# A two-layer hybrid-attention kernel: the products that feed its output projections are issued behind finished tiles

## The chip, the cores and the metric

The kernel runs on one core of one Trainium2 chip. The metric is the device time of one execution in microseconds (us), the median over several executions. Engines are named as the profile names them: PE (matrix multiply), DVE (vector), ACT (scalar activation), POOL (GpSimd) and SP, whose only work here is to issue DMA transfers.

## What is computed

The reference is a backbone of two layers over 2048 latent tokens and 256 context tokens, width 1024. Layer 0 runs windowed grouped-query attention beside latent attention, layer 1 neighbourhood attention on a grid. Both end in the same way, and only that end is touched by the change. Cut to it:

```python
o = attention(...)                     # (tokens, 1024), softmax denominators divided out
o = o * silu(z)                        # a gate path, the same width
h = h + gate * (o @ w_out)             # gate: one row for latent, one for context tokens
# after layer 1:  out = rms_norm(h, final_norm)
```

## The kernel before

`outp(l)` is the output projection of layer `l`. The attention stage has left three arrays in device memory, all laid out as channels by tokens: `o` as two halves that must be added, `z` (the gate values) and `rd` (reciprocals of the softmax denominators, one row for 64 channels). What the matmuls need is `(o_a + o_b) * rd * z`, split into a high part and a rest, for the 8 blocks of 128 channels.

The tokens are taken in chunks of 512: four and a half chunks in layer 0 (18 tiles of 128 tokens), four in layer 1 (16 tiles). `gsteps(c)` gives the steps for chunk `c`: `load(j)` issues, on SP, the transfers of block `j` (512 KB of `o`, 256 KB of `z`, twice 128 KB of `rd`), `ahead` says how many blocks the loads run in front, and `comp(j)` does the arithmetic: an add (L1188), a multiply by `rd` (L1189), a multiply by `z` (L1190), all on DVE, then a copy to the high part on ACT (L1192) and the rest on POOL (L1193). In chunk 0 of layer 1 the add and the first multiply run on POOL, since that chunk is prepared under the attention of layer 1. Layer 1 keeps its blocks in a ring of four buffers (`slots`), layer 0 in two or three buffers per array.

A tile is 48 matmuls (`product`, L1227: 8 blocks, three terms, two halves of the width) into one of four PSUM tiles `y`. A finished tile is multiplied by the gate (L1252) and added to the residual rows `rx` (L1253), both on DVE. In layer 0 SP then stores it (`s_h`, L1255). In layer 1 it is also normalised: squares with their sum on ACT (L1259), the root on POOL (L240, L241), a last multiply on DVE (L1261), then the store (L1262). In layer 0 DVE also works off the steps of `mod_rows` here (L207: products of `adat`, loaded through two buffers, with a row `scb`), which give the modulation of the next layer.

In the source the `comp`s of chunk `c+1` are spread over the tiles of chunk `c`. The order in which each engine issues them is not the source's: a scheduler picks, engine by engine, among the instructions that its own estimate says are ready. `tc.issue_after(x)` adds a rule to it: what is written under it comes behind `x` in the order of an engine, where both run on that engine. The hardware then follows that order strictly, with semaphores for the data.

The lines of the last context of layer 0's attention matter too: a reduction, a reciprocal and a small copy on DVE (L1061, L716 and `dnsb`, L720) make the last denominators, on which the last matmuls of chunk 0 wait.

## Time and profile before

| | us |
|---|---|
| time before, median of 3 runs | 3604.93 (3603.82 to 3609.08) |
| the profiled execution | 3600.51 |
| its span, first to last instruction | 3598.7 |
| PE busy in the span | 3452.3 (96%) |
| DVE / ACT / POOL busy | 2300.2 / 1901.1 / 1754.1 |

The profile is of one execution, so the times of a step are taken from it and the sum is set against its 3600.51 us. The span leaves out what lies before the first and behind the last instruction, 1.8 us. Line numbers of the rows are those of the kernel before.

### The profile page before, as it was taken

How to read it: one execution, taken by the hardware profiler on the slowest of the kernel's cores; microseconds unless marked ns; L12 is line 12 of the kernel's file. 1: busy time of each engine (PE TensorE's matmuls, PEld its weight loads, DVE VectorE, ACT ScalarE, POOL GpSimd, SP SyncE). 2: the span in 40 equal slices, each digit the busy share in tenths (PEclk: the TensorE clock that was granted, in tenths of full speed). 3: DMA queues.
4: the chain of work that ended last, by engine and by line, in shares of the span. 5: the costliest groups of instructions: out<-in, count | busy, mean ns of one | idle time of the engine just before them, and what ended most of it. 6: DMA issues, size and time to landing. Idle time of an engine off the chain costs nothing.

```text
span 3598.7 us, 53026 instructions
## 1 busy us (share of the span) xinstructions
PE 3452.3 (96%) x17607; PEld 2858.7 (79%) x17607; DVE 2300.2 (64%) x4305; ACT 1901.1 (53%) x3808; POOL 1754.1 (49%) x1656
## 2 busy tenths in 40 slices
PE   7899999999999999999989989999999999999988
PEld 6788878889877777777668768888888899999766
DVE  6545742489999999999968852203110188888565
ACT  4343432499777777777731132223222288888511
POOL 6465653211499999999962342224113134333532
PEclk9999999999999999999989989999999999999999
DMA  7757663852331232321269754544345567666685
GB/s 246 228 187 263 191 184 121 265 144 72 82 70 24 57 71 70 70 46 45 58 188 326 243 167 161 166 115 149 128 131 151 182 252 257 239 226 229 199 243 167
DMA packets 381052, 576.77 MB, mean 160 GB/s; under 512 B 35393, under 2 KB 218081, under 8 KB 370913
## 3 DMA queue, kind: packets, MB, share of 16 engines
q1 hardware_dynamic: 380777, 573.39, 52.2%
q8 instruction: 138, 2.26, 0.3%
q14 instruction: 137, 1.12, 0.1%
HBM read 399.36 MB, written 173.90 MB: 159 GB/s over the span
## 4 chain that ended last, share of the span: by engine, by line
PE 70%; DMA 9%; DVE 5%; issue 3%; ACT 2%; POOL 1%; SPq 1%; DVEq 0%; ACTq 0%; POOLq 0%
PE mm L276 7%; PE mm L278 7%; PE mm L277 7%; PE co L697 5%; PE ptc L688 4%; PE bo L1041 3%; PE bm L984 3%; PE bs L1020 3%; PE bo L1042 3%; PE bs L1021 3%; PE bs L1022 3%; PE ao L697 2%; PE pta L688 2%; DMA ord<-s_rd 1%; PE y L1227 1%
## 5 line engine op out<-in xcount | busy, mean ns | idle before, releaser
L270 POOL TENSOR_TENSOR wl<-ws,wh 128x512 fp32r<-128x512 f32 (+2 forms) x320 | 420.6, 1332 | 667.1 <-ACT wh L269 566.8
L1031 POOL TENSOR_TENSOR bacc<-bacc,bph 128x512 f32<-128x512 f32 (+1 forms) x528 | 667.4, 1266 | 34.5 <-ACT bph L1025 1.6
L1025 ACT ACTIVATE bph<-bs 128x512 fp32r<-128x512 f32 (+1 forms) x610 | 353.5, 579 | 214.8 <-PE bs L1022 183.0
L986 DVE TENSOR_REDUCE bmx<-bm 128x1 f32<-128x512 f32 (+1 forms) x656 | 406.0, 627 | 58.8 <-PE bm L984 42.4
L1027 DVE TENSOR_TENSOR bpl<-bs,bph 128x512 fp32r<-128x512 f32 (+1 forms) x610 | 400.1, 658 | 15.7 <-ACT bs L1026 14.8
L1026 ACT ACTIVATE bs<-bs 128x512 f32<-128x512 f32 (+1 forms) x610 | 350.8, 575 | 0.0
L276 PE MATMUL mm<-Uh,wh 128*128 128x512 f32 (+1 forms) x832 | 324.2, 391 | 4.6 <-ACT Uh L368 4.6
L1494 POOL TENSOR_TENSOR cbias<-cbu,rm 128x384 f32<-128x384 f32 x144 | 158.4, 1113 | 344.5 <-DVE cnm L1523 202.7
L277 PE MATMUL mm<-Ul,wh 128*128 128x512 f32 (+1 forms) x832 | 323.6, 389 | 0.0
L278 PE MATMUL mm<-Uh,wl 128*128 128x512 f32 (+1 forms) x832 | 321.3, 389 | 0.0
L1523 DVE CUSTOM_DVE_ANT_0 cp<-cs,cbias 128x640 f32<-128x640 f32 (+1 forms) x256 | 222.5, 886 | 138.6 <-PE cs L1519 91.9
L269 ACT ACTIVATE wh<-ws 128x512 fp32r<-128x512 f32 (+2 forms) x328 | 194.8, 613 | 207.8 <-DMA ws<-in_w_dram 174.3
L1041 PE MATMUL bo<-bph,bv 128*128 128x512 f32 (+1 forms) x610 | 240.4, 394 | 15.5 <-ACT bos L1046 15.5
L1020 PE MATMUL bs<-bqh,bkh 97*128 97x512 f32 (+1 forms) x610 | 242.5, 398 | 12.2 <-DVE bpl L1027 11.5
L249 DVE TENSOR_TENSOR plc<-ptc,phc 128x512 fp32r<-128x512 f32 (+1 forms) x384 | 234.8, 640 | 15.2 <-ACT phc L248 14.6
L984 PE MATMUL bm<-bkh,bqh 96*128 96x512 f32 (+1 forms) x656 | 241.4, 383 | 2.0 <-DVE bmx L986 1.7
L1042 PE MATMUL bo<-bpl,bv 128*65 128x512 f32 (+1 forms) x610 | 236.0, 387 | 3.3 <-DVE bos L1048 3.3
L1021 PE MATMUL bs<-bql,bkh 96*128 96x512 f32 (+1 forms) x610 | 238.3, 391 | 0.0
L1022 PE MATMUL bs<-bqh,bkl 96*128 96x512 f32 (+1 forms) x610 | 236.7, 388 | 0.0
L248 ACT ACTIVATE phc<-ptc 128x512 fp32r<-128x512 f32 (+1 forms) x384 | 205.4, 559 | 55.8 <-PE ptc L688 55.6
L1528 ACT ACTIVATE cp<-cp,cnm 128x640 f32<-128x640 f32 (+1 forms) x256 | 226.0, 883 | 16.2 <-DVE cnm L1523 15.8
L688 PE MATMUL ptc<-ident,cp 128*128 128x128 f32 x1408 | 205.4, 273 | 0.2 <-ACT cp L1528 0.2
(314 smaller groups left out, 8757.5 us busy)
## 6 DMA issues: line engine op xcount, KB each, us to landing
ws<-in_w_dram SPq DMA_DIRECT2D x256, 256.0 KB
ck<-s_kcT SPq DMA_DIRECT2D x32, 1152.0 KB
cv<-s_vc SPq DMA_DIRECT2D x64, 512.0 KB
adat<-in_adat_dram SPq DMA_DIRECT2D x96, 256.0 KB
o<-s_o SPq DMA_DIRECT2D x40, 512.0 KB
s_z<-zs SPq DMA_DIRECT2D x64, 256.0 KB
s_qcT<-st SPq DMA_DIRECT2D x64, 256.0 KB
s_kcT<-st SPq DMA_DIRECT2D x32, 512.0 KB
```

Of the source, the lines that this page charges most:

```text
L270: (eng or nc.gpsimd).tensor_sub(l[:, :w], s[:, :w], f(h[:, :w]))
L276: nc.tensor.matmul(out, a[0], b[0], start=first, stop=False)
L277: nc.tensor.matmul(out, a[0], b[1], start=False, stop=False)
L278: nc.tensor.matmul(out, a[1], b[0], start=False, stop=last)
L688: nc.tensor.transpose(ps[:, col : col + P], src(), ident)
L984: nc.tensor.matmul(ps[:, :w], t["qh"][0:96, b * P : (b + 1) * P], t["kh"][0:96, k0 : k0 + w], start=True, stop=True)
L986: nc.vector.tensor_reduce(t["mx"][:, j : j + 1], ps[:, :w], AX.X, ALU.max)
L1020: nc.tensor.matmul(ps[:, :n], t["kh"][0:97, ks], t["qh"][0:97, qs], start=True, stop=False)
L1025: nc.scalar.activation(hi[:, :n], ps[:, :n], AF.Exp)
L1026: self.acts = nc.scalar.activation(ps[:, :n], ps[:, :n], AF.Exp).ins
L1027: nc.vector.tensor_sub(lo[:, :n], ps[:, :n], f(hi[:, :n]))
L1031: self.pools = nc.gpsimd.tensor_add(st["acc"][:, :n], f((st["h0"] if j == 1 else st["acc"])[:, :n]), f(hi[:, :n])).ins
```

## The change

Three edits, all in `outp`:

```diff
-            ahead = (1 if l else 0, 2 if l else 1)
+            ahead = (1 if l else 0, 3 if l else 1)
+
+            done = []
...
-                    e1.tensor_add(a, a, o[:, 1, :n])
-                    e1.tensor_mul(a, a, rd[:, 0, :n])
-                    nc.vector.tensor_mul(a, a, z[:, 0, :n])
-                    h, lo = [x[:, j % 4, :n] for x in (G[c][0][j // 4], G[c][1][j // 4])]
-                    nc.scalar.activation(h, a, AF.Copy)
-                    nc.gpsimd.tensor_sub(lo, a, f(h))
+                    with ExitStack() as behind:
+
+                        for ins in done:
+                            behind.enter_context(tc.issue_after(ins))
+                        e1.tensor_add(a, a, o[:, 1, :n])
+                        nc.vector.tensor_mul(z[:, 0, :n], z[:, 0, :n], rd[:, 0, :n])
+                        nc.vector.tensor_mul(a, a, z[:, 0, :n])
+                        h, lo = [x[:, j % 4, :n] for x in (G[c][0][j // 4], G[c][1][j // 4])]
+                        nc.scalar.activation(h, a, AF.Copy)
+                        nc.gpsimd.tensor_sub(lo, a, f(h))
...
-                nc.vector.tensor_add(y, y, x)
+                done[:] = [nc.vector.tensor_add(y, y, x).ins]
...
-                    nc.scalar.activation(junk, y, AF.Square, accum_out=ss)
+                    done.append(nc.scalar.activation(junk, y, AF.Square, accum_out=ss).ins)
                     r = self.rstd(p, ss, D, "o")
-                    nc.vector.scalar_tensor_tensor(y, y, r, fg, ALU.mult, ALU.mult)
+                    done[0] = nc.vector.scalar_tensor_tensor(y, y, r, fg, ALU.mult, ALU.mult).ins
```

- A `comp` that the source writes behind a tile is now issued behind that tile's last DVE instruction (in layer 1 its ACT copy also behind the tile's squares). The `comp`s of chunk 0 stand ahead of any tile and are not tied.
- In layer 1 the loads of a chunk's blocks run three in front, not two.
- `z` is multiplied by `rd` first, then `o` by that product, both on DVE. In chunk 0 of layer 1 this takes eight multiplies from POOL to DVE. Elsewhere the count of instructions stays: 17609 rows on PE, 3322 on ACT and 2008 transfers before and after.

The scheduler answers with another order. In the changed kernel L1194, L1195 and L1196 are the add and the two multiplies, L1258 and L1259 the tile's gate and residual, L1267 the last multiply of layer 1. Names are the program's: `ry00` is tile 0 of layer 0, `oo010`, `oz010`, `ord010` the arrays of block 0 of chunk 1 of layer 0, `o114` block 4 of chunk 1 in layer 1.

DVE, layer 0, the last denominators of the attention stage. Before:

```order
L1061 TENSOR_REDUCE denb7_1536_21225<-bdt7_12_21226 128x4
L716 RECIPROCAL denb7_1536_21225<-denb7_1536_21225 128x4
L207 SCALAR_TENSOR_TENSOR mj1_000_21615,mcol0_21609<-adat1_0_0_21610,scb0_21606 128x512
L207 SCALAR_TENSOR_TENSOR mj1_010_21617,mcol0_21609<-adat1_0_0_21610,scb0_21606 128x512
L207 SCALAR_TENSOR_TENSOR mj1_100_21621,mcol0_21609<-adat1_1_0_21612,scb0_21606 128x512
L207 SCALAR_TENSOR_TENSOR mj1_110_21623,mcol0_21609<-adat1_1_0_21612,scb0_21606 128x512
L1188 TENSOR_TENSOR oo013_21564<-oo013_21564 128x512
L720 COPY dnsb7_1536_21235<-dnb7_1536_21233 4x128
```

The same place after:

```order
L1061 TENSOR_REDUCE denb7_1536_21225<-bdt7_12_21226 128x4
L716 RECIPROCAL denb7_1536_21225<-denb7_1536_21225 128x4
L207 SCALAR_TENSOR_TENSOR mj1_000_21615,mcol0_21609<-adat1_0_0_21610,scb0_21606 128x512
L207 SCALAR_TENSOR_TENSOR mj1_010_21617,mcol0_21609<-adat1_0_0_21610,scb0_21606 128x512
L207 SCALAR_TENSOR_TENSOR mj1_100_21621,mcol0_21609<-adat1_1_0_21612,scb0_21606 128x512
L207 SCALAR_TENSOR_TENSOR mj1_110_21623,mcol0_21609<-adat1_1_0_21612,scb0_21606 128x512
L207 SCALAR_TENSOR_TENSOR mj1_200_21627,mcol0_21609<-adat1_2_0_21619,scb0_21606 128x512
L720 COPY dnsb7_1536_21235<-dnb7_1536_21233 4x128
```

Nine instructions on blocks 0 to 2 of chunk 1 stood directly ahead of L1061 before; after, the last of chunk 0's stands there. Between L1061 and `dnsb` there are now five L207 and no block.

DVE, layer 0, the border from chunk 0 to chunk 1. Before:

```order
L1188 TENSOR_TENSOR oo017_21643<-oo017_21643 128x512
L1189 TENSOR_TENSOR oo017_21643<-oo017_21643,ord017_21645 128x512
L207 SCALAR_TENSOR_TENSOR mj1_500_21729,mcol0_21609<-adat1_5_0_21721,scb0_21606 128x512
L1190 TENSOR_TENSOR oo017_21643<-oo017_21643,oz017_21644 128x512
L207 SCALAR_TENSOR_TENSOR mj1_510_21731,mcol0_21609<-adat1_5_0_21721,scb0_21606 128x512
L1252 TENSOR_TENSOR ry00_21523<-y00_21376,gate0_21265 128x1024
L207 SCALAR_TENSOR_TENSOR mj1_600_21735,mcol0_21609<-adat1_6_0_21727,scb0_21606 128x512
L1188 TENSOR_TENSOR oo020_21822<-oo020_21822 128x512
L1252 TENSOR_TENSOR ry01_21560<-y01_21377,gate0_21265 128x1024
L1253 TENSOR_TENSOR ry00_21523<-ry00_21523,rx000_21366 128x1024
```

After:

```order
L1258 TENSOR_TENSOR ry00_21523<-y00_21376,gate0_21265 128x1024
L207 SCALAR_TENSOR_TENSOR mj1_1110_21912,mcol0_21609<-adat1_11_0_21816,scb0_21606 128x512
L1258 TENSOR_TENSOR ry01_21560<-y01_21377,gate0_21265 128x1024
L1259 TENSOR_TENSOR ry00_21523<-ry00_21523,rx000_21366 128x1024
L1194 TENSOR_TENSOR oo010_21527<-oo010_21527 128x512
L1195 TENSOR_TENSOR oz010_21528<-oz010_21528,ord010_21529 128x512
L1194 TENSOR_TENSOR oo011_21534<-oo011_21534 128x512
L1195 TENSOR_TENSOR oz011_21535<-oz011_21535,ord011_21536 128x512
L207 SCALAR_TENSOR_TENSOR mj1_1200_21916,mcol0_21609<-adat1_12_0_21908,scb0_21606 128x512
L1259 TENSOR_TENSOR ry01_21560<-ry01_21560,rx001_21368 128x1024
L1194 TENSOR_TENSOR oo012_21546<-oo012_21546 128x512
L1196 TENSOR_TENSOR oo010_21527<-oo010_21527,oz010_21528 128x512
```

Before, all 24 instructions on chunk 1's blocks stood ahead of the first finished tile. After, the first of them stands behind `ry00`'s residual add, and the high part of block 0 can be made only behind the last row shown. Ahead of the gate of `ry00` 12 L207 stood before and 23 stand after. The same pattern stands at the next borders (behind the gates of `ry04` and `ry05`, `ry08` and `ry09`, `ry012` and `ry013`). PE's order follows: before, the tiles from `y04` on are 48 matmuls in a row each; after, the tiles of a chunk take turns block by block. Behind the end of `y00` 18 matmuls of chunk 0 are left on PE (before and after), behind `y05` 34 of chunk 1, behind `y09` 27, behind `y013` 54.

SP, layer 1, the border from chunk 0 to chunk 1 (`rx102` and `rx103` are residual rows, `out_0_dram` the stores of finished tiles). Before, with the loads of `o114` to `o120` ahead of these rows:

```order
L1174 DMA o121_36991<-s_o1 128x2x512
L1175 DMA o121_36991<-s_z1 128x512
L1177 DMA o121_36991<-s_rd1 64x512 x2
L1174 DMA o122_36996<-s_o1 128x2x512
L1175 DMA o122_36996<-s_z1 128x512
L1177 DMA o122_36996<-s_rd1 64x512 x2
L1213 DMA rx102_36557<-s_h1 16x1024 x8
L1213 DMA rx103_36754<-s_h1 16x1024 x3
L1262 DMA out_0_dram<-ry10_36713 128x1024
L1213 DMA rx103_36754<-s_h1 16x1024 x5
L1262 DMA out_0_dram<-ry11_36763 128x1024
```

After:

```order
L1179 DMA o113_36739<-s_rd1 64x512
L263 DMA wso171_36524<-in_wo1_dram 128x512
L1219 DMA rx102_36557<-s_h1 16x1024 x8
L1268 DMA out_0_dram<-ry10_36713 128x1024
L1219 DMA rx103_36749<-s_h1 16x1024 x8
L1268 DMA out_0_dram<-ry11_36758 128x1024
L1176 DMA o114_36769<-s_o1 128x2x512
L1177 DMA o114_36769<-s_z1 128x512
L1179 DMA o114_36769<-s_rd1 64x512 x2
L1176 DMA o115_36779<-s_o1 128x2x512
L1177 DMA o115_36779<-s_z1 128x512
```

The loads of blocks 4 to 7 of chunk 1 and 0 to 2 of chunk 2 stood ahead of the first store; they stand behind the second now. From there to the last block SP issues 20 blocks, 8 groups of residual rows and 8 stores. On DVE the order there is, after: gates and residuals of `ry10` and `ry11`, L1267 of `ry10`, add and multiply of `o110`, L1267 of `ry11`, adds and multiplies of `o111` to `o113`, and then the second multiply of `o110`. On PE 38 matmuls of chunk 0 followed the end of `y10` before, 37 after. Behind the last block of chunk 3, PE has 136 matmuls left.

## Rows read from the trace of the kernel before

**Rows 1.** The page's first line and its busy time by engine.
```profile
span 3598.7 us, 53026 instructions
...
PE 3452.3 (96%) x17607; PEld 2858.7 (79%) x17607; DVE 2300.2 (64%) x4305; ACT 1901.1 (53%) x3808; POOL 1754.1 (49%) x1656
```

**Rows 2.** Busy time, clock (PEclk), DMA share, GB/s by stretch, layer 0.
```profile
1870.00:1880.00 10.00, 8.54 (x26) 6.79 (x27) 9.76 (x16) 1.78 (x3) 5.00 (x3) 0.66 0.90 297
1880.00:2030.00 150.00, 150.00 (x645) 120.61 (x643) 122.76 (x210) 17.41 (x30) 35.58 (x28) 1.00 0.98 314
2030.00:2060.00 30.00, 24.98 (x116) 20.42 (x116) 25.06 (x45) 8.73 (x16) 15.34 (x15) 0.94 0.62 211
```

**Rows 3.** The same view, layer 1: attention (first row) and output projection.
```profile
3000.00:3300.00 300.00, 297.18 (x2179) 277.54 (x2177) 260.06 (x545) 261.08 (x566) 101.53 (x92) 1.00 0.68 235
...
3420.00:3440.00 20.00, 18.79 (x81) 14.51 (x80) 14.17 (x17) 4.31 (x7) 8.08 (x7) 1.00 1.05 294
3440.00:3460.00 20.00, 20.00 (x87) 15.97 (x86) 14.24 (x15) 4.72 (x8) 10.24 (x10) 1.00 0.82 219
...
3490.00:3500.00 10.00, 2.92 (x6) 1.68 (x6) 5.22 (x6) 1.78 (x3) 2.34 (x3) 0.57 0.95 247
```

**Rows 4.** Waits, 1840 to 2060 us: engine and line, its releaser, total, times, longest.
```profile
DVE mj L207 <- DMA adat<-in_adat_dram: 14.7, 7, 4.0
...
PE ft L360 <- DVE fx L332: 5.0, 3, 3.5
PE y L1227 <- DVE dnsb L720: 4.9, 1, 4.9
```

**Rows 5.** Waits, 3380 to 3600 us.
```profile
DVE o L1189 <- DMA o<-s_rd: 44.1, 13, 17.2
...
PE y L1227 <- ACT Gql L1192: 11.8, 2, 8.8
```

**Rows 6.** Timeline of TensorE, 1864 to 1874 us.
```profile
1871.46 1.22 PE L1227 MATMUL y<-who,Gqh 128*128 128x512 f32 x2 [4.91 <-DVE dnsb L720]
```

**Rows 7.** Timeline of VectorE, 1858 to 1874 us.
```profile
1863.16 0.18 DVE L716 RECIPROCAL denb<-denb 128x4 f32<-128x4 f32 x1
...
1868.24 1.62 DVE L207 SCALAR_TENSOR_TENSOR mj<-adat,scb 128x512 bf16<-128x512 f32 x1
...
1871.13 0.27 DVE L720 COPY dnsb<-dnb 4x128 f32<-4x128 f32 x1
```

**Rows 8.** Timeline of TensorE, 1888 to 1900 us.
```profile
1897.82 0.74 PE L1227 MATMUL y<-who,Gg 128*128 128x512 f32 x2
```

**Rows 9.** Groups by line: durations in ns as min/median/max, first and last start.
```profile
L1188 DVE TENSOR_TENSOR oo<-oo x32: 409/683/1776, 1849.9 to 2020.4; 128x512 f32<-128x512 f32 x24, 128x256 f32<-128x256 f32 x8
...
L1227 PE MATMUL y<-who,Gg x512: 387/393/628, 1897.8 to 3588.7; 128*128 128x512 f32 x171
...
L1192 ACT ACTIVATE Gg<-o x16: 617/632/635, 3393.6 to 3551.7; 128x512 fp32r<-128x512 f32 x16
...
L1193 POOL TENSOR_TENSOR Gg<-oo,Gg x16: 1282/1295/1757, 1864.7 to 1992.5; 128x512 fp32r<-128x512 f32 x16
...
L1252 DVE TENSOR_TENSOR ry<-y,gate x34: 1208/1217/1227, 1896.6 to 3589.1; 128x1024 f32<-128x1024 f32 x34
...
L1259 ACT ACTIVATE oj<-ry x16: 1056/1058/1060, 3438.2 to 3591.7; 128x1024 bf16<-128x1024 f32 x16
...
L1261 DVE SCALAR_TENSOR_TENSOR ry<-ry,rstdo,fg x16: 1273/1284/2317, 3442.2 to 3593.8; 128x1024 f32<-128x1024 f32 x16
```

**Rows 10.** Timeline of TensorE, 3425 to 3438 us.
```profile
3434.62 0.62 PE L1227 MATMUL y<-who,Gg 128*128 128x512 f32 x2
3435.08 0.62 PE L1227 MATMUL y<-wlo,Gg 128*128 128x512 f32 x2
```

**Rows 11.** Timeline of TensorE, 3484 to 3506 us.
```profile
3496.74 1.22 PE L1227 MATMUL y<-who,Gql 128*128 128x512 f32 x2 [8.83 <-ACT Gql L1192]
```

**Rows 12.** Timeline of VectorE, 3424 to 3446 us.
```profile
3433.24 1.22 DVE L1252 TENSOR_TENSOR ry<-y,gate 128x1024 f32<-128x1024 f32 x1
```

## The prediction

> **What bounds it now.** I read the page first: PE is busy for 96% of a span of 3598.7 us [rows 1]. So a change elsewhere counts only where PE waits, or is made to wait. The table of stretches shows where it does. In layer 0's projection PE is full from 1880 on for 150 us, at full clock; it loses time ahead of that, in 1870 to 1880, and behind it [rows 2]. In layer 1's it is full at first and loses time in 3490 to 3500, where it is busy 2.92 us of 10 [rows 3]. The waits name the releasers: in layer 0 4.9 us for `dnsb`, the copy of the last denominators, and 5.0 us for `fx`, already the next stage [rows 4]; in layer 1 11.8 us for a high part (L1192), while DVE's multiply by `rd` waited 44.1 us for its transfers [rows 5]. The transfers matter in both: DMA share is 0.98 over those 150 us of layer 0, and 0.82 to 1.05 in layer 1's projection [rows 2, 3].
>
> In layer 1 the old order hurts DVE too. `y10`'s gate could start when `y10` ended. The first matmul of chunk 1 started at 3434.62, and the next pair 0.46 later, so a matmul takes 0.23 [rows 10]; 38 matmuls stood between, so `y10` ended at 3434.62 - 8.7 = 3425.9. The gate began at 3433.24 [rows 12], 7.3 us late, behind blocks that waited for transfers. PE did not feel it, since those blocks were for PE.
>
> **The change, step by step.** Durations: a block's operation on DVE 0.69 us, the copy to the high part 0.63, POOL's rest 1.30, gate and residual 1.22 each, squares 1.06, last multiply 1.28 [rows 9]; L207 0.77 with its accumulator, by the nearest row up to 1.62 when POOL works beside it [rows 7].
>
> *Start of layer 0.* `dnsb` ran at 1871.13, though its reciprocal had been done since 1863.3 [rows 7]; PE then waited 4.91 us and restarted with a pair of 1.22 us, about twice the usual [rows 6]. The reciprocal stood behind nine operations on blocks whose loads were late, and `dnsb` behind four L207 and a block. Now five L207 stand there and no block. Those need a third `adat` tile, so not all is won. All of it would be 4.91 us and some 2.5 of slow matmuls, nothing if `adat` holds it as long: 0 to -7.5, I take **-5**.
>
> *Border of chunks 0 and 1, layer 0.* Before, chunk 1's first matmul followed chunk 0's last with no wait [rows 8]: its blocks lay ready. Now block 0 waits for tile 0. From the end of `y00`, DVE does gate 1.22, L207 0.77, gate 1.22, residual 1.22, four block operations 2.76, L207 0.77, residual 1.22, two more block operations 1.38; ACT adds 0.63. That is 11.2 us. PE has 18 matmuls left, 4.1 us. It waits **+7.1**. From below +4, if gates start early; from above +11, if four of DVE's operations meet POOL's (1.78 in place of 0.69, the longest row of L1188 [rows 9]), or if the 23 L207 now ahead of the gate, whose `adat` comes through two buffers and was waited for 14.7 us in the old order [rows 4], make it late. Later blocks come in time: four tiles share a block on PE, 24 x 0.23 = 5.5 us, and a block costs DVE 2.1.
>
> *The next borders.* The same chain counts from `y05`, `y09` and `y013`, with part of its first gate and L207 done already: some 10.6 us. PE has 34, 27 and 54 matmuls, 7.8, 6.2 and 12.4 us. Waits: **+2.8**, **+4.4** and none; bounds 0 and +10 together, at both ends as above.
>
> *The clock.* PE falls to about half speed after a wait. The wait of 4.91 left a granted clock of 0.66 in its stretch [rows 2, 6], the one of 8.83 left 0.57 and pairs of 1.22 [rows 3, 11]; after waits of at most 3.5 the stretch of 30 us shows 0.94 [rows 2, 4]. A mean of 0.66 over 10 us is 6.8 us at the half level; the wait itself was 4.91 of those 10 us, and about 5 us of matmuls at half speed lose 2.5. I count one such loss, at the first border, **+2.5**, bounds 0 and +7.5. The Trainium skill (TensorE: Matmul & The Clock Gate, HAM oscillation — how this bites in real kernels) tells of bursts that each wait for data and each restart at the half clock; by it every one of the three new waits would pay, and the sum would be 5 us more. The rows of 4.91 and 8.83 agree with it, that of 3.5 only weakly.
>
> *Into the next stage.* All tiles' last stores and `fx` come later against PE, but the three waits there (5.0 us in all [rows 4]) may shrink in turn: **0**, bounds -5 and +5.
>
> *Layer 1, chunk 0.* Eight multiplies leave POOL for DVE (8 x 0.69 = 5.5 us) under attention, where PE is busy 99% and DVE 87% of the time [rows 3]: **0**. Without PE's cover it would cost the 5.5.
>
> *Layer 1, the borders.* From `y10`'s end: two gates and two residuals 4.9; the residual of `ry10` is done at 3.7, squares and root take about 3 more (the first squares began at 3438.2, the first last multiply 4.0 later [rows 9], with DVE busy at its end), so that the last multiply ends at 8.0; two block operations 1.4; last multiply 1.28; six block operations 4.1; the second multiply 0.7; ACT 0.63: 16.1 us. PE is free after 37 matmuls, 8.5. It waits 7.6 us, where it waited for nothing. In return DVE no longer sits on transfers, and the later borders are covered (48 matmuls or more follow the chain's start).
>
> But the loads are late now. Block 4's buffer is that of block 0, free when POOL has made its rest: 16.1 + 1.3, at 3443.3. Before, seven blocks had been issued by then. From there to the last block go 20 blocks of 1.05 MB and 16 residual tiles and stores of 0.52: 29.4 MB. At the best stretch's 294 GB/s that is 100 us, at 219, the lowest, 134 [rows 3]. The nearest row is the lowest, since it holds residuals and stores as well as blocks; but its share was 0.82, so the engines had room, and a share of 1 makes 219 into 267: I take 110 us. The last block is then ready at 3443.3 + 110 + 3 for landing and arithmetic = 3556.3; 136 matmuls, 31.3 us, follow: 3587.6. Before, the last matmul ended at 3589.1 [rows 9]. So **-1.5**; +22.5 at 219, -11.5 at 294. If the loads never bind, chunk 1 starts at 3442.0 and three chunks of 192 matmuls (44.2) end at 3574.6: -14.5.
>
> *Sum.* -5 + 7.1 + 2.8 + 4.4 + 2.5 + 0 + 0 - 1.5 = +10.3. Against the profiled 3600.5 that is 3610.8. The median of the runs, 3604.9, lies 4.4 above the profiled one, so I predict **3615.2**. Of a change under 0.2%, 7.2 us, I say that it can't be told from none.
>
> **Rivals.**
> 1. *Faster: layer 1's loads keep ahead.* DVE finishes tiles at once and PE's waits there go. With layer 1 at -14.5 and the start at -7.5, and layer 0's borders at half their price since gates start before the last tile of a group ends (+7), the sum is -15: 3590. With those two it decides where layer 1 gives 6.7 or more, the 29.4 MB in 105 us, 280 GB/s. For it: 294 was reached with blocks alone, and layer 0 moved 314 over 150 us of blocks, residuals, stores and `adat` [rows 2]. Against: in the stretches that hold residuals and stores as well it was 219 and 247 [rows 3]. The Trainium skill (DMA: Bandwidth & Descriptors, Specifications) gives a core some 358 GB/s from device memory; by it the loads would not bind. No row of layer 1 here comes near that. Chance 0.22.
> 2. *No change that can be measured.* The loads at 294 (-11.5), the rest as in the sum without a clock loss: 10.3 + 1.5 - 2.5 - 11.5 = -2.2, 3602.7. Chance 0.2.
> 3. *Much slower.* The loads at 219 (+22.5), layer 0 as summed: 10.3 + 1.5 + 22.5 = +34.3, 3639. For it: 219 is what the stretch right behind the first border ran at [rows 3], with PE at no wait. Chance 0.13.
>
> My forecast, border waits in layer 0 and a layer 1 that gives about nothing, has 0.45: alone it spans 3606 to 3628.
>
> **How the numbers follow.** Faster is rival 1: 0.22. Same is rival 2 with the forecast's low tail: 0.23. Slower is the rest of the forecast and rival 3: 0.55. The range runs from 3591, which holds rival 1 down to nearly its price, to 3636, short of rival 3's; what it leaves out is half of each, 0.17 or so.
>
> **What would show it.** Right: PE waits for L1192 of some 7 us where chunk 1 begins in layer 0, of 2 to 5 at the next two borders, released by DVE's multiplies; a clock under 1 behind the first; no 4.91 for `dnsb`; in layer 1 a wait of 7 to 8 at chunk 1, then DMA share near 1 and waits for L1188's transfers up to chunk 3. Wrong: PE as full as before from 1880 to 2030, or the waits of layer 1 gone behind chunk 1 with DMA share under 0.8. The prediction fails most likely on the pace of layer 1's loads, which no row gives for this order, and next on the L207s ahead of the first gate.

## The result and the profile after

The changed kernel takes 3660.80 us (median of 5 runs, 3656.28 to 3665.47), the kernel before, run beside it, 3603.82. The ratio on record is 1.0163, with a 95% interval of 1.0148 to 1.0177: **slower by some 57 us**. (The ratios here and below are those on record; they are not quotients of the medians printed beside them.) The prediction had the sign, but the time lies above its range (3591 to 3636). The profiled execution after took 3665.21 us, 64.7 more than that of before; the traces are compared against this difference.

The page's first line and the busy time by engine, as in [rows 1]:
```profile
span 3663.4 us, 52959 instructions
...
PE 3469.3 (95%) x17607; PEld 2867.4 (78%) x17607; DVE 2296.3 (63%) x4313; ACT 1900.1 (52%) x3808; POOL 1744.8 (48%) x1648
```
PE issues the same 17607 matmuls in 3469.3 us in place of 3452.3: 17 us went into slower matmuls (some 5 in layer 0's projection and 6 in layer 1's), and the rest of the 64.7 is waiting. DVE has eight operations more and POOL eight less, the multiplies of layer 1's chunk 0. In this kernel L1194 is the add, L1195 the multiply by `rd`, L1196 the last multiply of a block, L1198 ACT's high part, L1199 POOL's rest, L1233 the product, L1258 the gate and L1259 the residual.

I cut both traces at the same matmuls. The start is a segment's first matmul, the last column the difference:

| from, to | before | after | |
|---|---|---|---|
| layer 0's projection: first product, first on a chunk-1 block | 53.0 | 57.3 | +4.3 |
| from there to its last product | 167.1 | 175.5 | +8.4 |
| from there to the next stage's first product (L276) | 0.2 | 30.2 | **+30.0** |
| the next stage, up to layer 1's attention output | 802.1 | 800.3 | -1.8 |
| layer 1's attention output | 527.1 | 532.7 | +5.6 |
| from there to the first product on a chunk-1 block | 40.3 | 45.1 | +4.8 |
| from there to the last product | 154.1 | 168.0 | **+13.9** |

With what lies before (-0.5) that is the 64.7. Two rows hold two thirds of it.

**Layer 0.** PE's waits from 1840 us to the next stage's first product (releaser, total, times, longest), to set against [rows 4]:
```profile
PE ft L360 <- DVE fx L332: 15.8, 3, 11.4
PE y L1233 <- ACT Gg L1198: 14.9, 2, 10.9
PE mm L276 <- ACT Uh L368: 8.2, 1, 8.2
PE y L1233 <- ACT Gqh L1198: 6.7, 1, 6.7
...
PE y L1233 <- DVE dnsb L720: 0.5, 1, 0.5
```
The second and fourth rows are the new border waits, and the 4.91 for `dnsb` has become 0.5. The first and third are not in projection 0 at all: they are the next stage, waiting for its first input rows. The timeline of TensorE gives each border wait its place:
```profile
1901.57 1.22 PE L1233 MATMUL y<-who,Gg 128*128 128x512 f32 x2 [10.91 <-ACT Gg L1198]
...
1955.66 1.22 PE L1233 MATMUL y<-who,Gqh 128*128 128x512 f32 x2 [6.75 <-ACT Gqh L1198]
...
2007.39 1.22 PE L1233 MATMUL y<-who,Gg 128*128 128x512 f32 x2 [3.99 <-ACT Gg L1198]
```
They are the borders 0 to 1, 1 to 2 and 2 to 3. Each wait is followed by a pair of 1.22 us, where a pair took 0.62 to 0.74 before [rows 8, 10]. The stretches show it as well (columns as in [rows 2]):
```profile
1880.00:1900.00 20.00, 10.66 (x46) 8.27 (x44) 16.18 (x35) 0.00 (x0) 0.00 (x0) 0.83 0.45 143
1900.00:1940.00 40.00, 38.43 (x155) 31.02 (x156) 31.69 (x54) 6.04 (x9) 12.13 (x8) 0.91 0.99 326
1940.00:1960.00 20.00, 13.25 (x49) 10.36 (x48) 15.18 (x24) 1.19 (x2) 3.32 (x2) 0.78 0.64 205
...
2090.00:2110.00 20.00, 5.95 (x20) 4.30 (x20) 17.04 (x18) 8.98 (x17) 17.26 (x13) 0.50 0.46 146
```
The 150 us without a gap, at clock 1.00 and a DMA share of 0.98 [rows 2], are gone. The worst stretch is the last: PE busy for 5.95 us of 20 at a clock of 0.50, the lower of its two levels (1.2 GHz).

What holds the next stage up stands on the DMA queue (SP) and on POOL. The next stage's first load is issued at 2069.46, after SP stood idle for 2.9 us:
```profile
2065.94 0.58 SPq L1261 DMA_DIRECT2D s_h<-ry  x1
2069.46 0.80 SPq L323 DMA_DIRECT2D fx<-s_h  x2
```
```profile
2068.43 1.00 POOL L1199 TENSOR_TENSOR Gkl<-oo,Gql 128x256 fp32r<-128x256 f32 x1 [3.08 <-ACT Gql L1198]
```
```profile
SPq L323 <- POOL Gkl L1199: 2.9, 1, 2.9
```
POOL's third of the four rests `Gkl`, that of the last chunk's last block but one, ends at 2069.43, 0.03 us ahead of the issue, and the queue's waits of 2064 to 2070 us name it as the releaser (last row). DVE's multiply of the last block, which an expectation below names, still ran at that time:
```profile
2068.87 0.85 DVE L1196 TENSOR_TENSOR oo<-oo,oz 128x256 f32<-128x256 f32 x1
```
The kernel before shows the same pair, 0.02 us apart, the rest ending at 2023.32 and the load going at 2023.34:
```profile
2022.30 1.02 POOL L1193 TENSOR_TENSOR Gkl<-oo,Gql 128x256 fp32r<-128x256 f32 x1 [3.85 <-ACT Gql L1192]
```
```profile
2023.34 1.85 SPq L323 DMA_DIRECT2D fx<-s_h  x2
```
So this load has always followed the work on the last blocks. Its tile takes memory that the blocks of the projection give back; a run below tests that. Before, the load was 42 us ahead of the projection's last product, and the next stage's transposes (L360) ran between products. Now it is 8 us ahead.

**Layer 1.** The stretches around the border (columns as in [rows 3]):
```profile
3445.00:3465.00 20.00, 18.05 (x77) 13.84 (x76) 0.00 (x0) 3.30 (x6) 7.09 (x6) 1.00 0.72 214
3465.00:3485.00 20.00, 14.40 (x62) 11.29 (x61) 13.00 (x16) 3.72 (x7) 5.19 (x6) 0.97 0.36 115
...
3487.00:3625.00 138.00, 116.64 (x451) 87.58 (x450) 86.00 (x94) 25.64 (x43) 47.74 (x43) 0.90 0.87 228
```
At the border DMA share is 0.36; in the stretch around the border before it was 1.05 [rows 3]. The DMA queue says why:
```profile
3461.83 0.47 SPq L1179 DMA_DIRECT2D o<-s_rd  x1
...
3474.61 3.57 SPq L1219 DMA_DIRECT2D rx<-s_h  x8
...
3486.72 0.38 SPq L1176 DMA_DIRECT2D o<-s_o  x1
```
From 3461.83 to 3486.72 no block is loaded: the ring's four buffers are full, and their blocks wait for `y10`. (The residual rows at 3474.61 are no blocks.) VectorE's timeline shows when that ended:
```profile
3470.84 1.23 DVE L1258 TENSOR_TENSOR ry<-y,gate 128x1024 f32<-128x1024 f32 x1 [30.47 <-PE y L1233]
```
PE waits 5.99 us for the first block of chunk 1, and it waits again at the later borders, longest at the one to chunk 2:
```profile
3485.39 1.22 PE L1233 MATMUL y<-who,Gg 128*128 128x512 f32 x2 [5.99 <-ACT Gg L1198]
...
3551.90 1.22 PE L1233 MATMUL y<-who,Gql 128*128 128x512 f32 x2 [5.65 <-ACT Gql L1198]
```
From chunk 1's first product on, PE is busy for 146.3 us where it was 139.9 (before, then after), so 6.4 of the 13.9 us are slower matmuls:
```profile
3435.00:3589.00 154.00, 139.85 (x576) 110.88 (x574) 97.06 (x95) 27.89 (x47) 41.16 (x48) 0.93 0.73 206
```
```profile
3485.00:3653.00 168.00, 146.25 (x574) 111.58 (x575) 97.87 (x102) 29.43 (x50) 51.23 (x50) 0.91 0.76 204
```

### The profile page after: what moved, and what is told of

It is laid out like the page before. It is cut to its first block, busy times and chain, and to the rows that moved or that the text cites. A ratio compares the mean times of both kernels' runs of the same rounds, so it can differ in the third digit from the quotient of the medians.

```text
span 3663.4 us, 52959 instructions
## 1 busy us (share of the span) xinstructions
PE 3469.3 (95%) x17607; PEld 2867.4 (78%) x17607; DVE 2296.3 (63%) x4313; ACT 1900.1 (52%) x3808; POOL 1744.8 (48%) x1648
## 4 chain that ended last, share of the span: by engine, by line
PE 70%; DMA 8%; DVE 5%; issue 3%; ACT 2%; POOL 2%; SPq 1%; DVEq 0%; ACTq 0%; POOLq 0%
PE mm L278 7%; PE mm L277 7%; PE mm L276 7%; PE co L697 4%; PE ptc L688 4%; PE bo L1041 3%; PE bs L1020 3%; PE bm L984 3%; PE bs L1021 3%; PE bs L1022 3%; PE bo L1042 3%; PE y L1233 2%; DMA adat<-in_adat_dram 2%; PE ao L697 2%; PE pta L688 2%
## 5 line engine op out<-in xcount | busy, mean ns | idle before, releaser
L1027 DVE TENSOR_TENSOR bpl<-bs,bph 128x512 fp32r<-128x512 f32 (+1 forms) x610 | 400.6, 658 | 15.8 <-ACT bs L1026 15.0
L276 PE MATMUL mm<-Uh,wh 128*128 128x512 f32 (+1 forms) x832 | 325.2, 392 | 8.2 <-ACT Uh L368 8.2
```

The lines of the kernel that those rows point to most:

```text
L276: nc.tensor.matmul(out, a[0], b[0], start=first, stop=False)
L1027: nc.vector.tensor_sub(lo[:, :n], ps[:, :n], f(hi[:, :n]))
```

## The experiments

Theory A: the tie is the whole loss, by three ways: waits at the borders, the next stage's loads that stand behind the last tied blocks, and layer 1's loads that stand behind the border. Rival B: layer 1's bandwidth alone (the prediction's third rival), with layer 0 worth about ten us. Rival C: the multiply moved to DVE costs as much as the tie. The three runs first are the parts one by one. "Start" below means the time from layer 0's first product to the next stage's first one: 220.3 us before, 263.0 after.

**Tie in layer 0 alone.** The two other edits are taken back.
```
                        for ins in done if l == 0 else []:
```


> The kernel before with the tie alone, and in layer 0 alone (loads in layer 1 and the multiplies as before). Theory: the tie in layer 0 costs twice, some 12 us in waits at the borders of its chunks and some 28 us behind it, because the next stage's first loads and transposes, which ran under the last 40 us of the projection, now start at its end: +40 us, the next stage's first weight matmul about 40 us later, layer 1 as before. Rival: the tie costs only the border waits, and the 28 us come from the multiplies or from layer 1: +12 us.

Measured: 3649.03 us, ratio 1.0135 (1.0117 to 1.0152). Start 268.8, of which 32.0 lie between the projections' last and the next stage's first product; layer 1's attention 529.5 and its projection 154.3 as before. The next stage's first load again follows POOL's rest of the last block but one (ended at 2074.87), at 2074.90. That is 47 us slower, where 40 was expected. Rival B falls: most of the loss is in layer 0 and behind it.

**Tie in layer 1 alone.**
```
                        for ins in done if l == 1 else []:
```


> The kernel before with the tie alone, and in layer 1 alone (two blocks ahead, multiplies as before). Theory: layer 1's loads wait behind finished tiles, and their pace of about 220 GB/s then sets the end: +15 to +20 us, all of it behind the last attention matmul of layer 1. Rival: only the border wait of 5 to 8 us counts, the rest of layer 1's loss comes from three blocks ahead or from the order of the multiplies: +5 to +8 us, or a gain, since DVE finishes tiles sooner.

Measured: 3621.14 us, ratio 1.0051 (1.0031 to 1.0071). Start 218.2; layer 1's border 45.5 and its projection 172.4, which is 18.3 more than before, as the theory had it. The stretch ahead of its border shows the stop of the loads, with a share of 0.31:
```profile
3395.00:3415.00 20.00, 18.51 (x80) 14.47 (x79) 0.00 (x0) 3.90 (x7) 7.64 (x6) 1.00 0.83 241
3415.00:3435.00 20.00, 17.42 (x75) 13.73 (x74) 9.98 (x11) 4.34 (x8) 7.79 (x8) 1.00 0.31 103
```

**The multiply alone.** Gate times reciprocal first, on DVE in layer 1's chunk 0; no tie.
```
-                    e1.tensor_mul(a, a, rd[:, 0, :n])
+                    nc.vector.tensor_mul(z[:, 0, :n], z[:, 0, :n], rd[:, 0, :n])
```


> The kernel before with the gate times reciprocal first, on DVE, and nothing else. Theory: in chunk 0 of layer 1 the multiply on DVE waits for its transfer and holds up attention's own work behind it: +5 us, between the first and the last attention matmul of layer 1. Rival (what the prediction said): hidden under TensorE, within 2 us of before.

Measured: 3604.43 us, ratio 1.0003 (0.9990 to 1.0016). Rival C falls for the time. But layer 1's attention is 531.7 long, 4.6 more, and its wait for DVE grew (waits of 2860 to 3440 us):
```profile
PE co L697 <- DVE plc L249: 9.4, 7, 3.2
```
It was 5.0 in 3 waits before; other segments were shorter by as much (1 to 4 us each), so no loss can be seen in the time.

**The multiply back on POOL, with the tie.**
```
-                        nc.vector.tensor_mul(z[:, 0, :n], z[:, 0, :n], rd[:, 0, :n])
+                        e1.tensor_mul(z[:, 0, :n], z[:, 0, :n], rd[:, 0, :n])
```


> The changed kernel with chunk 0's multiply of gate and reciprocal in layer 1 on GpSimd, where its first multiply was before. Theory: the multiply on VectorE waits for its transfer and holds attention's work: the time from the first to the last attention matmul of layer 1, 532.7 in the changed kernel, falls to 528 to 530. Rival: scatter; it stays at 532 to 534.

Measured: 3653.10 us, ratio 1.0147 (1.0129 to 1.0166); attention 526.6, 6.1 shorter than after, with the wait for `plc` at 5.6. Over all profiled runs attention takes 526.6 to 530.5 without the multiply on DVE (13 runs, mean 528.7) and 530.5 to 534.9 with it (7 runs, mean 532.6). About 4 us are its price there; the time alone would not show it, since this interval overlaps that of after.

**Where the loss of layer 0 sits.** Three cuts: chunk 4 untied, otherwise as after; the tie in chunks 1 and 2 only, layer 0 alone; and the tie held to the tile before the last finished one, layer 0 alone.
```
                        for ins in done if l or c < 4 else []:        # first
                        for ins in done if l == 0 and c < 3 else []:  # second
                        for ins in prev if l == 0 else []:            # third; prev[:] = done ahead of each new tile
```


> The changed kernel without the tie for chunk 4 of layer 0, the half chunk whose products are made under chunk 3. Theory: what delays the next stage is that chunk 4's loads stand late on SP, ahead of the next stage's; untied they go earlier, and 15 to 28 us of the 57 come back, with the next stage's first transposes again between the projection's matmuls. Rival: the next stage is late because the tiles of chunks 1 to 3 end late or take turns on TensorE; then it stays within 5 us of the changed kernel.

> The kernel before with the tie alone, in layer 0, for the blocks of chunks 1 and 2 alone. Theory: the border waits of these two chunks stay, some 10 us, and the next stage gets its cover back as far as chunks 3 and 4 held it up: with the tie on chunk 4 lifted (the run before) 12.5 of 30 us were left there, and lifting chunk 3 as well should leave under 8. Together +10 to +18 us. Rival: what is left comes from the late end of the earlier tiles or from tiles that take turns on TensorE; then 12 us or more stay there and the run is +22 us or more.

> The kernel before with the tie alone, in layer 0, but each block's work behind the tile before the last one (one tile of slack). Theory: the first blocks of a chunk are ready at its border, so the border waits of some 12 us go to under 4; the loads of chunk 4 and of the next stage still stand late on SP, so 20 to 30 us stay there: +22 to +34 us, against +47 with the tie itself. Rival: border waits cause the delay of the next stage; then both go and the run is within 8 us of before.

Measured: 3644.37 (1.0116; 1.0101 to 1.0131), 3637.86 (1.0079; 1.0062 to 1.0096) and 3623.39 us (1.0042; 1.0027 to 1.0057). Starts 247.2, 247.3 and 237.4. In the first the start is shorter than the changed kernel's by 15.8, as expected. The second comes out as its rival: 29.5 us slower than before, where 10 to 18 were expected, and 12.1 us of the gap ahead of the next stage stay though chunks 3 and 4 are free. Whether the tiles that end late or the tiles that take turns on PE hold their work back was not separated. The third tells most: its border waits are all but gone, its projection is no longer than before (216.5 against 220.1), and still the next stage's first product comes 20.9 us behind the last product and its start is 17.1 longer. The run is 15 us slower than before, less than the 22 expected. The first loads of the next stage, in this order:
```profile
2046.96 0.80 SPq L323 DMA_DIRECT2D fx<-s_h  x2
```
```profile
2060.59 0.80 SPq L323 DMA_DIRECT2D fx<-s_h  x2
```
```profile
2051.23 0.80 SPq L323 DMA_DIRECT2D fx<-s_h  x2
```
The next stage's first products came at 2080.7, 2094.4 and 2085.0: 33.7 to 33.8 us behind the load each time (37.8 in after). Each time the load goes 0.02 to 0.03 us behind POOL's rest of the last block but one, as above. Two pairs of tiles must be loaded, normed and transposed in turn through two buffers, so the second pair's loads follow the first pair's transposes. In these runs, then, a load that is issued less than 34 us ahead of the projection's last product leaves PE without products for the difference: 13 us ahead (third) gives 20.9, and 21 and 22 ahead (first and second) 12.7 and 12.1.

**The next stage's memory moved.** The same ties as in the change, but two pools are allocated in the other order, so that the first input rows don't take the blocks' memory.
```
-            gp = self.pool(ctx, f"o{l}g", 1)
             lp = self.pool(ctx, f"o{l}l", 3)
+            gp = self.pool(ctx, f"o{l}g", 1)
```


> The changed kernel with two pools of the output projection allocated in the other order, so that the next stage's input rows take over the memory of chunk 1's and 3's products and not that of the block buffers. Theory: the next stage's first loads waited for the last block's multiply because they take over its buffer; now they go when chunk 3's last tile has been read, some 12 to 15 us earlier, and the 30 us between the projection's last matmul and the next stage's first weight matmul fall to 15 to 20. Rival: they wait for something else; 27 to 32.

Measured: 3645.03 us, ratio 1.0123 (1.0106 to 1.0141). The first load is issued at 2055.34, 24.2 us ahead of the projection's last product in place of 7.6, and the next stage is 18.8 us late, not 30.2; the start is 252.3, shorter by 10.7. So the memory holds the load in the change, since the ties are the same. Here the load no longer waits for POOL. It goes out 0.1 us behind a tile's store:
```profile
2054.77 0.47 SPq L1261 DMA_DIRECT2D s_h<-ry  x1
2055.34 1.45 SPq L323 DMA_DIRECT2D fx<-s_h  x2
```
So its place in SP's order, behind the stores and the loads of chunk 4, holds it now, by this trace, still 32 us later than before; no run tests that. Why the next stage's first product comes 43.0 behind it, in place of 34 to 38, was not followed.

**Layer 1 without the residual rows' transfers.** The change, and the kernel before, with the rows of layer 1's first two tiles used for all: 14 tiles of 512 KB aren't loaded, and the sums are of other rows.
```
+                    X[(c2, t2)] = X[work[n % 2]] if l else res(chunks[c2][0] + t2 * P, c2, t2)
```


> The changed kernel, but in layer 1 the residual rows are loaded for the first two tiles only and used again for the others (so the residual of those is another's): 7 MB and 112 of SP's transfers fewer. Theory: behind the first border of layer 1 the pace of its loads sets the end, so from chunk 1's first matmul to the last it takes 10 to 14 us less than the 168 of the changed kernel. Rival: the order on VectorE sets it; within 4 us of 168.

> The kernel before with the same saving in layer 1 (residual rows of the first two tiles used for all). Theory: there too the loads set layer 1's end, so the 154 us from chunk 1's first matmul to the last fall by 8 to 15, near the 133 that three chunks of matmuls take without a wait. Rival: within 4 us of 154.

Measured: 3636.34 (1.0074; 1.0059 to 1.0089) and 3582.26 us (0.9925; 0.9910 to 0.9939). Layer 1's projection behind the border falls to 136.7 and 133.1, three chunks of 44.2 almost without a gap: 31 and 21 us less, where 10 to 14 and 8 to 15 were expected. So nearly all that either kernel loses there is waiting for transfers, and with 7.3 MB less even the tied order keeps PE fed. In the second of them the DMA engines' share is near 1 and then falls, the work done:
```profile
3460.00:3480.00 20.00, 20.00 (x88) 16.22 (x87) 18.75 (x21) 5.84 (x11) 8.64 (x9) 1.00 1.03 292
3520.00:3540.00 20.00, 20.00 (x88) 16.29 (x87) 12.05 (x10) 3.45 (x6) 2.25 (x7) 1.00 0.21 87
```

**Chunk 1 of layer 1 untied.**
```
                        for ins in done if l == 0 or c > 1 else []:
```


> The changed kernel without the tie for chunk 1 of layer 1. Theory: the loads of that chunk's later blocks go out ahead of the first tiles again, so the lost 50 us or so of early loading come back: the first border's wait goes and chunk 1's first to the last matmul takes 154 to 160 us, against 168. Rival: the pace of SP and of the transfers behind the border sets the end whatever went out early; 165 to 168.

Measured: 3652.39 us, ratio 1.0140 (1.0125 to 1.0155); border 41.1, projection 159.2. With loads that run on over the first border (the first of the 20 blocks goes 20.9 us behind the end of attention, 46.4 in the changed kernel), 12.8 us of the 18.7 come back.

**The form of the row transfers.** A tile of residual rows is 8 transfers of 64 KB. I took them for the brake, and tried in the kernel before: contiguous rows in one transfer (other rows than the right ones), the same 8 on ACT's queue, and on POOL's.
```
-                    for r in range(8):
-                        nc.sync.dma_start(x[r * 16 : r * 16 + 16, :], src[r, c * 16 : c * 16 + 16, :])
+                    nc.sync.dma_start(x, scr["h1"][a : a + P, :])     # first; second: nc.scalar, third: nc.gpsimd
```


> The kernel before, with the residual rows of a tile of layer 1 loaded in one transfer of 128 rows that lie side by side (not the tile's own rows, so the residual is another's): the same bytes, 16 transfers in place of 128. Theory (SP's queue): layer 1's loads were slow because eight small transfers of SP for each tile stand ahead of the blocks, so the 154 us fall to 133 to 140, as without these loads. Rival (bytes): it is the 512 KB of each tile that count; 150 us or more.

> The kernel before, with the residual rows of layer 1 loaded from ScalarE's queue, the same transfers and bytes. If SP's queue is the limit: 8 to 20 us faster than before, though ScalarE's high-part copies then stand behind these transfers and may take some of it back. If bytes are: within 5 us of before.

> The kernel before, with the residual rows of layer 1 loaded from GpSimd's queue, the same transfers and bytes. If SP's queue is the limit: 8 to 20 us faster than before, less what GpSimd's rests lose behind them. If bytes are: within 5 us of before.

Measured: 3597.25 (0.9974; 0.9960 to 0.9987), 3605.51 (1.0010; 0.9998 to 1.0021) and 3631.39 us (1.0078; 1.0061 to 1.0095). Border and projection: 57.4 and 133.2; 47.7 and 150.8; 59.3 and 158.6 (before 40.3 and 154.1). The run on ACT's queue stays within 5 us of before, as it was to if SP's queue is not the limit. One transfer seemed to take the projection to its floor, but the border grew by 17.1.

**The right rows in one transfer**, in the kernel before; the same with the tie in layer 1; the same with layer 1's weights put ahead of the blocks; and in the whole change.
```
-                    for r in range(8):
-                        nc.sync.dma_start(x[r * 16 : r * 16 + 16, :], src[r, c * 16 : c * 16 + 16, :])
+                    nc.sync.dma_start(x, src[:, c * 16 : c * 16 + 16, :])
...
+                    with tc.issue_after(self.wdma) if l and c == 1 else ExitStack():   # third run alone, around a block's loads
```


> The kernel before with the residual rows of a tile of layer 1, its own rows, in one transfer in place of eight. As in the run with rows that lie side by side: 133 to 140 us from chunk 1's first matmul to the last in place of 154, but 10 us or more lost ahead of it, since the weights of the projection now stand behind more blocks: 0 to -10 us in all.

> The tie in layer 1 alone together with the residual rows in one transfer. If what made the tie slow there is the pace of these transfers, it costs nothing now but its border wait of 5 us, and the weights stand ahead of the late blocks: 133 to 140 us behind the border, 10 to 17 us faster than before in all. If the tie is slow whatever the transfers: over 150 there, and slower than before.

> The kernel before, with each tile of layer 1's residual rows in one transfer, and the loads of layer 1's chunk 1 held until the last weight load of the projection has been issued. If the 64 KB transfers set the pace of layer 1's projection, and the lost 25 us of the run with one transfer were the weights alone: attention's end to the first matmul of chunk 1 back to 40 to 46 us, the projection behind it 133 to 140 us, and a time of 3582 to 3592. If blocks that start some 12 us later are missed: the border at 40 to 46 and the projection at 145 to 155, a time like before's. If the weights are late for another reason (their three staging buffers): a border of 55 to 65 again and a time of 3600 to 3608.

> The changed kernel whole, with each tile of layer 1's residual rows in one transfer. If the tie's order holds layer 1 back by itself, as the run with the tie in layer 1 alone showed: projection from the first matmul of chunk 1 on 160 to 167 us, border 50 to 58, and a time of 3655 to 3665. If the transfers were the larger part: projection 135 to 145, a time of 3630 to 3642.

Measured, with border, projection and their sum:

| | us | ratio (95%) | border | projection | sum |
|---|---|---|---|---|---|
| before | 3603.8 | | 40.3 | 154.1 | 194.4 |
| one transfer | 3606.54 | 1.0011 (0.9999 to 1.0022) | 65.0 | 134.0 | 199.0 |
| with the tie in layer 1 | 3620.67 | 1.0051 (1.0034 to 1.0069) | 56.9 | 164.3 | 221.2 |
| weights first | 3613.14 | 1.0030 (1.0018 to 1.0041) | 43.4 | 158.2 | 201.6 |
| the change, one transfer | 3660.08 | 1.0156 (1.0142 to 1.0169) | 51.1 | 157.0 | 208.1 |

My guess of the brake falls: none of these runs is faster than before, as the first was expected to be. With one transfer the weights come late, and PE waits for them (waits of 3380 to 3700 us):
```profile
PE y L1226 <- ACT who L269: 20.5, 3, 11.3
```
Those 20 us gave the blocks the lead that made the projection short: 11 of the 20 were issued ahead of chunk 1's first product, 6 before. Put the weights first, and the border is 43.4 again, but the blocks start late:
```profile
3402.72 20.88 SPq L263 DMA_DIRECT2D wso<-in_wo_dram  x7
3423.66 0.43 SPq L1175 DMA_DIRECT2D o<-s_o  x1
```
PE then waits 8.54 us in the middle of the projection. Without the tie it is 191 to 202 us from the end of attention to the last product, whatever the form and the order (190.6, 194.4, 198.5, 199.0, 201.6; POOL's queue apart, 217.9; runs that leave layer 1 as it was have 194.4 to 198.6); only fewer bytes made it much shorter (176.8). In the whole change one transfer did raise the pace, over nearly the same stretch as above:
```profile
3487.00:3620.00 133.00, 115.45 (x452) 89.80 (x453) 92.48 (x101) 26.58 (x44) 51.07 (x44) 0.92 0.84 246
```
246 GB/s at a share of 0.84 is 293 at a full one, against 228 / 0.87 = 262. The border grew by 6.0 at the same time, and the time is that of the change. No version with the right rows beats the kernel before; the one run below it with all its bytes, 0.9974, added other rows.

The Trainium skill (DMA: Bandwidth & Descriptors, Why a DMA increments its semaphore by 16 and not by 1) lets the slowest dimensions of the two sides set how many engines a transfer uses; by it the right rows, eight groups of 16, would use fewer than contiguous ones. The projections of 134.0 and 133.2 don't show a difference, but the sums do (199.0 and 190.6), and so do the ratios, whose intervals lie apart (1.0011 and 0.9974). No run here counted engines, and the two runs read different rows, so the cause of it is open.

## Why the prediction was wrong

**Start of layer 0: right.** -5 was predicted; the wait for `dnsb` fell from 4.9 to 0.5, and the slow pair behind it is gone.

**Layer 0's borders: right in place, too small.** Predicted 7.1, 2.8, 4.4 and none at 3 to 4; measured 10.91, 6.75, 3.99 and none. Sum 21.6 against 14.3, at the upper bound for the first and 0.7 above the joint bound of 10 for the next two. The chain itself was right: from the gate of `ry00` to chunk 1's first product it is 10.2 us, where 11.2 was summed. What came on top is what the text gave as a reason for its upper bound, the L207 ahead of the gate: DVE waited 10.0 us for `adat` ahead of it (waits of 1878 to 1903 us), and the gate began some 4.9 us after `y00` had ended (18 products of 0.23 ahead of 1890.65). At the next border it was one wait of 4.82:
```profile
DVE mj L207 <- DMA adat<-in_adat_dram: 10.0, 6, 6.3
```
```profile
1891.35 1.22 DVE L1258 TENSOR_TENSOR ry<-y,gate 128x1024 f32<-128x1024 f32 x1
...
1944.82 0.69 DVE L207 SCALAR_TENSOR_TENSOR mj<-adat,scb 128x512 bf16<-128x512 f32 x1 [4.82 <-DMA adat<-in_adat_dram]
```

**The clock: one loss was counted, three came.** Each of the three borders restarts with a pair of 1.22 us. From 1840 us to the next stage's first product PE's 215.1 us of work became 220.0, with the slow pair for `dnsb` gone: some 5 net, where 2.5 stood in the sum. The Trainium skill's rule (TensorE: Matmul & The Clock Gate, HAM oscillation — how this bites in real kernels), by which all three waits would pay, agrees with these rows. The sum gave it as 5 us more. Layer 1's 6.4 us of slower matmuls stood in no term.

**"Into the next stage: 0, bounds -5 and +5": the step that failed.** I set the next stage's waits against the 5.0 us of `fx` [rows 4], and did not ask what its load waited for. It was tied by memory to POOL's rest of the last block but one, and the blocks were what the change moved. Its first load went from 42 us ahead of the projection's last product to 8, with a chain of at least 34 us behind it. The waits for transposes and for `Uh` are 24.0 us in place of 5.0, and the transposes themselves no longer stand between products. The run with one tile of slack shows this loss almost by itself: border waits gone, the start 17.1 us longer. With other memory alone 10.7 us of the start came back; the rest of it stands in SP's order, by that run's trace, and was not tested.

**Layer 1's chunk 0: small, not nothing.** The multiplies were priced at 0 under attention. They cost about 4 us, since DVE is a releaser of `plc` there; the mean share of 87% [rows 3] hid that PE waits for it.

**Layer 1's border: right.** The block loads were to start again 17.4 us behind `y10`'s end. `y10` ended at 3470.8, where its gate began, and they started at 3486.7, 15.9 behind. PE's wait was 5.99, predicted 7.6.

**The pace of layer 1's loads: mis-sized, as the text feared.** "A share of 1 makes 219 into 267" took the 29.4 MB at 267 GB/s. They ran at 228, 129 us in place of 110: 19 more. So -1.5 became +18.7, near the upper bound of 22.5. What failed is the share: it was 0.87, not 1. The rate at a full share was right (262). The trace of the kernel before held the answer, had the mean over these 20 blocks been read and not the best and the lowest stretch. Their stretch before, and after:
```profile
3416.00:3540.00 124.00, 110.94 (x459) 87.91 (x458) 77.56 (x81) 23.53 (x39) 41.23 (x40) 0.93 0.87 237
```
```profile
3487.00:3609.00 122.00, 103.52 (x409) 79.07 (x408) 72.17 (x80) 22.59 (x38) 39.01 (x38) 0.91 0.87 228
```
The first and the last of the 20 were issued here, before:
```profile
3416.05 0.39 SPq L1174 DMA_DIRECT2D o<-s_o  x1
...
3538.82 0.53 SPq L1174 DMA_DIRECT2D o<-s_o  x1
```
After, it was at 3486.72 and 3607.51. That is 122.8 us before and 120.8 after: the tie did not slow the loads. It made them start 46.4 us behind the end of attention in place of 21.7, and of these 24.7 us 6.0 were made up by the end of the projection. The claim that the later borders of layer 1 are covered fell with it (5.65 us at chunk 2). What keeps the share at 0.87, with the tie and without, no run shows.

**Sum.** The terms with their measured sizes: borders, clock and start of layer 0 some 22 (21.6 + 5 - 4.4); next stage some 20 (the 42.7 of the start less those 22); layer 1's attention 5.6; border and projection 18.7. That is 67, less 1.8 in the next stage and 0.5 ahead of the projection: 64.7. In the timed runs the two ties alone cost 1.35% and 0.51%, together 0.23% more than the change as a whole. The traces show where: the tie in layer 0 alone has a start of 268.8, and five runs with the whole change in layer 0 have 261.0 to 263.6; the tie in layer 1 alone has border and projection of 217.9, the change 213.1. So under the ties the other edits give 5 to 6 us back in each of these stretches, by one run each; in layer 0 that can only be the order of the multiplies. Why was not followed.

Rival 3, "much slower, loads at 219", came nearest, for layer 1's part of it. Rival 1 named 280 GB/s as the point from which it decides; the stretch behind the border stayed at 228. The forecast's sign was not luck, since the border waits came where it put them; but +10.3 of 64.7 left out its largest part.

## What to carry to other kernels

When a change delays the last use of a buffer, look for what takes over its memory, in the next stage too. An issue that goes out 0.02 to 0.03 us behind the end of an operation on tiles that it has nothing to do with, in one run after the other, is such a tie, and the waits of the DMA queue name the releaser. The chain behind it (34 us here) must fit ahead of the end. When work that frees the buffers of the next loads is put behind a finished tile, the loads start later; whether they catch up is read from their mean pace in the old kernel (237 GB/s here), not from its best stretch (294). And a border that grows while the stretch behind it shrinks is a lead moved, not time won: compare the sum of the two.

## What was not expected of the hardware

The DMA share alone doesn't give the pace, and the form of the transfers didn't settle what a full share is worth. In the changed kernel it was 262 GB/s with residual rows in pieces of 64 KB and 293 with the same rows in pieces of 512 KB, in nearly the same stretch. In the kernel before it went the other way: 237 / 0.87 = 272 over the 20 blocks with pieces of 64 KB, 240 / 0.93 = 258 with pieces of 512 KB:
```profile
3405.00:3532.00 127.00, 105.74 (x422) 83.48 (x423) 72.02 (x78) 25.14 (x43) 51.11 (x45) 0.89 0.93 240
```
The same 64 KB pieces issued from ACT's queue left the time as it was (1.0010), and from POOL's queue made it longer by 0.8%.
